# Two mixers' output projections in another order, with six of eight couples by seven products, in a float32 encoder trunk on one NeuronCore

## The chip, the cores and the metric

The program runs on one core of a Trainium2 chip. The metric is the device time of one execution in microseconds (us). The kernel before took 2365.94 us, the median of three runs (2365.79, 2365.94 and 2369.58). A further execution was recorded by the hardware profiler.

## What is computed

A two-layer encoder trunk over 256 tokens with model width 2048, in float32. Layer 0 mixes tokens with a bidirectional mLSTM (8 heads), layer 1 with a bidirectional HGRN2 (16 heads). Each mixer ends in an output projection, and a gated MLP of width 5504 follows:

```python
for layer in range(DEPTH):
    hn = rmsnorm(h, norm_mix_g[layer])
    mix = mlstm_mixer(hn, ...) if layer % 2 == 0 else hgrn_mixer(hn, ...)   # ends in y @ w_out
    h = h + mix
    h = h + conv_glu(rmsnorm(h, norm_ffn_g[layer]), ...)   # (gelu(conv(a)) * v) @ w_down, [a, v] = hn @ w_up
return rmsnorm(h, final_g)
```

The change concerns `y @ w_out` (a 256x2048 by 2048x2048 product, once in each layer), the residual add and the norm behind it, and the first product of the MLP.

## The kernel before

**Products.** Every large product is split into float32r parts: an operand `x` becomes `xh + xl`, a weight `wh + wl`, and three matmuls (h by h, h by l, l by h) stand for one float32 product. ScalarE (ACT) casts a raw weight piece to `wh` (L147), VectorE (DVE) subtracts to get `wl` (L148); a piece is 128x1024. TensorE (PE) runs a list of *chunks* one after another (`stream`, L324 on): "tm" chunks make 256 tokens by 512 columns (L373), "fm" chunks make 256 features by 256 tokens (L357 for h, L361 for l), and "st" chunks (*pairs*, L236) make 256 tokens by 1024 columns.

**Seven products.** A pair takes its k-tiles two at a time, as *couples* `u`: a 2x2 by 2x2 block product of 128x128 by 128x512 blocks. Directly that is eight block products, 24 matmuls of 128x512. For the couples listed in `seven`, it is done in seven block products, 21 matmuls, by a scheme of Strassen's kind. It needs four sums of blocks of `x` (`token_sums`, tiles `sx`, made on DVE and ACT) and four differences T1 to T4 of weight blocks. The eight accumulators hold four PSUM banks "mm" (P1, P6, P7, P5) and four "aux" (C11, C12, C21, C22). After the last couple by seven, `mid` (L581 on) adds P1, P6, P7, P5 to the residual `hm`; after the last couple, `done` adds C11 to C22 (L598).

**Weight differences.** They are made in one of two ways. `combine` (L202 on) makes them on DVE inside the pair (L207, four subtractions of 128x512). `prepare` (L613 on) makes them long before: it loads a couple of blocks into tiles `praw` (L621 or L395), subtracts four times (L633) and stores the result to DRAM `tscr` (L636); the pair then loads 768 KB into a tile `T` (L198), 768 KB of raw blocks (L135) and 256 KB from `tscr` (L199). `T` comes from `temporary`, with three buffers in the MLP's pool "ff" and two in the output projection's pool "op". A tile `T` is read by a cast and a subtraction of 1024 columns and by one of 512 columns, with one raw piece between.

**Who prepares what.** Each mixer stage prepares couples ahead (`prepare_early`): in layer 0 six, all for the MLP's first pair (`FIRST = 6`); in layer 1 nine, three for the mixer's own pair and six for the MLP. There the loads and stores go through the queue of SyncE (SP). The other couples of the MLP are prepared while its "up" chunks run; there loads and stores go through GpSimd (POOL). In all 63 couples are prepared; nine are combined inside a pair, three of them in layer 0's mixer, six in the MLPs (`FLY`).

**The output projection.** `mixed` (L656 on) makes four blocks of 512 columns of the residual: chunk `c0` (columns 0 to 511, tm), the pair `two` (columns 512 to 1535, couples 2, 4, 6 by seven, the other five by eight), then `c3` (columns 1536 to 2047, tm). The mixer's pool is closed and the pool "op" is opened when `c0` is done; "op" is closed before `c3`, and "ff" opens at the first up chunk.

**The norm behind it.** When a block of 512 columns of `hm` is complete, `Norm.add` (L420 on) squares it on ACT and queues `turn`: eight PE transposes in two groups (L434, tiles `pz`), then ACT and DVE split the four k-tiles `xt` (L379, L380). A `turn` that meets a running pair waits for it, or, where the pair has `ends`, for `mid`. After the fourth block the norm is finished (L417 to L460). The first up chunk needs `xt` 0 to 15 in order of k.

**Order.** The program text is turned into a queue of instructions for each engine by a list scheduler that simulates the engines at compile time; what is marked by `pin` or `late` keeps its program order on its engine. Side jobs (norms, preparations, heads of the mixers) are advanced by a clock `side.tick`, whose units are about 1 us in a tm chunk and about 0.54 us in an fm chunk. On the chip each engine runs its queue strictly in order.

Of the kernel before, what the change touches and what calls it, by code (L numbers as in the profile page):

```python
# [8 lines left out]
F32 = mybir.dt.float32  # L9
# [3 lines left out]
ALU = mybir.AluOpType  # L13
PSUM = bass.MemoryType.PSUM

P = 128
T = 256
D = 2048
KT = D // P
FT = 5504 // P  # L20
# [30 lines left out]
FLY = (2,), (5,), (2,), ()  # L51
FIRST = 6
SPLIT = (0, 2, 5), (0, 2, 5)
END = 3
SCRATCH = 4096
SEVEN_MIX = (2, 4, 6)

# [9 lines left out]
def trunk_kernel(ctx, tc, xT, x_d, fg_d, pp_d, cst_d, w_gate, w_first, w_aq, w_ak, w_av, w_ao, w_aout, w_ao2,  # L67
                 w_bq, w_bv, w_bg, w_bout, w_bo2, w_up, w_d0, w_d1, w_d3, out, mscr, tscr):
    nc = tc.nc
# [326 lines left out]


    class Norm:

        def __init__(self, gname, goff):  # L400
            self.g, self.o = gname, goff
            self.xs, self.rc_, self.R_ = [None] * KT, None, None

# [21 lines left out]
        def turn(self, c):  # L425
            yield 2.5
            while held and not held[-1].rest:
                yield 1.0
            for k0 in (4 * c, 4 * c + 2):
                pz = psm.tile([P, 512], F32, tag="mm", name="pz") if held else aux("pz")  # L430
                for k in (k0, k0 + 1):
                    for t in range(2):
                        o = (k - k0) * T + t * P
                        pe.transpose(pz[:, o:o + P], hm[:, t, k * P:(k + 1) * P], ident)  # L434
                for k in (k0, k0 + 1):
                    self.take(k, pz[:, (k - k0) * T:(k - k0 + 1) * T])
                yield 1.0
            if c == 3:
                self.total()
                self.finish()  # L440
                self.spread()
# [30 lines left out]
        def x(self, k):  # L472
            side.until(lambda: self.xs[k] is not None)
            return self.xs[k]

    class FinalNorm:
# [136 lines left out]
    def prepare(tiles, todo, first, period, finished, start, ahead):  # L613

        loaded = []

        def load(i):
            if i < len(todo):
                r = tiles(i)
                for j in range(2):  # L620
                    start(r[j], todo[i][0][:, j * 1024:(j + 1) * 1024])  # L621
                loaded.append(r)

        put = start if ahead else nc.sync.dma_start
        yield first
        load(0)
        if ahead:
            load(1)
        for i, (_, dst) in enumerate(todo):
            yield period / 2  # L630
            B11, B22, B21, B12 = (loaded[i][j // 2][:, j % 2 * 512:(j % 2 + 1) * 512] for j in range(4))
            for x, y, out in ((B12, B22, B22), (B12, B11, B12), (B11, B22, B11), (B21, B11, B21)):
                dve.tensor_tensor(out, x, y, ALU.subtract)  # L633
# [3 lines left out]
            if ahead:  # L637
                load(i + 2)
            yield period / 3
            if not ahead:  # L640
                load(i + 1)
        finished.append(True)
# [3 lines left out]
    def prepare_early(mp, layer, first, period):  # L646
        todo, finished = early[layer]
        side.push(prepare(lambda i: [mp.tile([P, 1024], F32, tag=f"p{j}", name="praw") for j in range(2)],
                          todo, first, period, finished, late, False))

# [4 lines left out]

    def mixed(w, w2, x, norm, close, layer=None):  # L656

        c0, _, _, c3 = project(lambda c: w[c // 3], KT, x, norm)
        op, SX, first = ExitStack(), {}, c0.done

        def sums(u):
            side.until(lambda: u in SX)
            return SX[u]

        two = pair(w2, KT, 1, x, sums, norm, SEVEN_MIX)
        if layer is not None:
            for u in SEVEN_MIX:
                store(two, w2, u, early[layer][0])
            two.waits = [early[layer][1]]

        def token():
            for i, u in enumerate(SEVEN_MIX):
                f = temporary(two.pool, "f")
                for j in range(2):
                    y = x(2 * u + j).bitcast(F32)
                    dve.tensor_tensor(f[:, j * T:(j + 1) * T], y[:, 0:T], y[:, T:2 * T], ALU.add)
                SX[u] = token_sums(two.pool, i, f[:, 0:T], f[:, T:2 * T], f[:, 2 * T:4 * T])
                yield 5.0

        def done(ps):  # L680
            side.drain()
            close()
            two.pool = op.enter_context(tc.tile_pool(name="op", bufs=1))
            two.pool.tile([P, LEAD], F32, name="lead")
            first(ps)
            side.push(token())

        c0.done, c3.before = done, op.close
        return [c0, two, c3]


    def mlstm(norm, nxt):
# [10 lines left out]
        box = {}  # L703
# [184 lines left out]
        for pr in range(AH // 2):  # L888
# [36 lines left out]
            def done_first(ps, done_v=done_v):  # L925
# [10 lines left out]
                side.push(start(gs))  # L936
                prepare_early(box["mp"], 0, 62.0, 25.0)

# [30 lines left out]

        return chunks + mixed(w_aout, w_ao2, yx, nxt, stack.close)  # L970


    def hgrn(norm, nxt):
# [4 lines left out]
        def begin():  # L978
            mp = box["mp"] = stack.enter_context(tc.tile_pool(name="hg", bufs=1))
            box["lv"] = mp.tile([P, 2 * P], F32, name="lv")  # L980
            late(box["lv"][:, 0:FINE * QUAD], cst_d[:, C_LV:])
            prepare_early(mp, 1, 30.0, 38.0)
            box["turn"] = 0
# [194 lines left out]
    def ffn(layer, norm, nxt):  # L1178
# [40 lines left out]
        for part, (f0, nf) in enumerate(((0, FA), (FA, FB))):  # L1219
# [96 lines left out]
def layout(x, norm_mix_g, norm_ffn_g, mlstm_w_in, mlstm_b_gate, mlstm_head_g, mlstm_w_out, hgrn_w_in, hgrn_lb,  # L1316
# [45 lines left out]
def build(nc, ins, out_shape=(2, P, D), **kw):  # L1362
# [3 lines left out]
    mscr = nc.dram_tensor("mscr", (64, T), F32, kind="Internal").ap()  # L1366
    tscr = nc.dram_tensor("tscr", (len(SEVEN_MIX) + 2 * sum(len(s) for layer in SEVEN for s in layer), P, 2048), F32, kind="Internal").ap()
    with tile.TileContext(nc, schedule_with_timeline_sim=True) as tc:
# [17 lines left out]
```

## Time and profile before

| | |
|---|---|
| median of three runs | 2365.94 us |
| the profiled execution | 2365.23 us |
| its span, first to last instruction | 2363.5 us |
| around the span | 1.7 us |
| mean granted TensorE clock | 0.999 |
| DMA traffic | 632.98 MB, mean 268 GB/s |

The span runs in stages: the first mixer to 299 us, its output projection to 388 us (`c0`, the pair from 322 to 364, `c3`), the MLP of layer 0 to 1081 us, the second mixer with its projection to 1664 us (the pair from 1597 to 1640), the MLP of layer 1 to the end. Times in the views are counted from the span's start. A PE row gives the duration of a single matmul from its start to its modelled end; matmuls overlap, so the pace of a series is read from starts, not from durations.

### The profile page before, as it was taken

The numbers are of one execution on the slowest core, as the hardware profiler recorded it, in microseconds if no ns is written. First come the engines' busy times: TensorE is split into PE (matmuls) and PEld (weight loads), VectorE is DVE, ScalarE is ACT, GpSimd is POOL, SyncE is SP. The second block draws the span as 40 slices with busy tenths as digits, with TensorE's granted clock in tenths as the row PEclk, the third lists the DMA queues.
The fourth block names the chain that finished last, engine by engine and source line by source line (L and its number), as shares of the span: only waits on it lengthen the run. The fifth ranks groups of instructions, "written<-read, shape, count | busy, mean of one in ns | idle before, by whom it ended". The sixth has DMA issues, their size and how long they took to land.

```text
span 2363.5 us, 38477 instructions
## 1 busy us (share of the span) xinstructions
PE 2353.8 (100%) x14545; PEld 2016.3 (85%) x14545; DVE 1992.4 (84%) x3087; ACT 1470.9 (62%) x2340; POOL 296.6 (13%) x436
## 2 busy tenths in 40 slices
PE   9999999999999999999999999999999999999998
PEld 8888888888888888888888888888888888888887
DVE  7777688997899998897888888778898789889787
ACT  7655455555665555676777777776555566455565
POOL 0100002110001110000232322221110000211000
PEclk9999999999999999999999999999999999999999
DMA  8776658985689996796656666557997588899695
GB/s 306 236 250 240 214 196 297 374 309 196 215 322 357 352 346 224 265 326 224 213 203 222 216 218 211 204 173 271 347 353 248 191 297 330 315 347 349 201 356 200
DMA packets 122267, 632.98 MB, mean 268 GB/s; under 512 B 13776, under 2 KB 14928, under 8 KB 77664
## 3 DMA queue, kind: packets, MB, share of 16 engines
q1 hardware_dynamic: 92736, 525.83, 62.7%
q0 software_dynamic: 28768, 103.89, 12.4%
q8 instruction: 114, 1.87, 0.3%
q10 hardware_dynamic: 576, 0.79, 0.1%
q14 instruction: 73, 0.60, 0.1%
HBM read 562.24 MB, written 68.22 MB: 267 GB/s over the span
## 4 chain that ended last, share of the span: by engine, by line
PE 98%; DVE 1%; issue 0%; DMA 0%; ACT 0%; POOL 0%; SPq 0%; POOLq 0%; DVEq 0%
PE mm L357 37%; PE mm L361 19%; PE mm L373 18%; PE pc L236 12%; PE mm L236 8%; PE pn L852 1%; PE py L1111 1%; PE pd L1061 0%; DVE wl L148 0%; PE pa L1061 0%; PE pz L434 0%; DMA raw<-in_w_first 0%; PE S L838 0%; ACT wh L147 0%; PE pz L1132 0%
## 5 line engine op out<-in xcount | busy, mean ns | idle before, releaser
L357 PE MATMUL mm<-xt,wh 128*128 128x512 f32 x3776 | 1312.4, 394 | 0.0
L148 DVE TENSOR_TENSOR wl<-raw,wh 128x1024 fp32r<-128x1024 f32 (+1 forms) x844 | 1037.1, 1234 | 231.0 <-ACT wh L147 224.0
L147 ACT CAST wh<-raw 128x1024 fp32r<-128x1024 f32 (+1 forms) x844 | 876.2, 1043 | 521.5 <-PE mm L357 307.1
L361 PE MATMUL mm<-xt,wl 128*128 128x256 f32 x3776 | 1043.4, 278 | 0.0
L357 PEld LDWEIGHTS mm<-xt,wh 128*128 128x128 f32 x3776 | 705.7, 188 | 161.1 <-issue 0.4
L361 PEld LDWEIGHTS mm<-xt,wl 128*128 128x128 f32 x3776 | 709.3, 188 | 4.5
L373 PE MATMUL mm<-wh,xt 128*128 128x512 f32 x1024 | 324.1, 392 | 0.2
L236 PE MATMUL pc<-wh,g 128*128 128x512 f32 (+1 forms) x716 | 243.1, 388 | 0.0
L373 PEld LDWEIGHTS mm<-wh,xt 128*128 128x128 f32 x1024 | 191.2, 188 | 39.4 <-ACT wh L147 0.5
L633 DVE TENSOR_TENSOR praw<-praw 128x512 f32<-128x512 f32 x252 | 173.4, 690 | 37.1 <-DMA praw<-in_w_d 28.0
L373 PE MATMUL mm<-wl,xt 128*128 128x512 f32 x512 | 199.9, 391 | 0.1
L236 PEld LDWEIGHTS pc<-wh,g 128*128 128x128 f32 x716 | 134.1, 188 | 27.9 <-ACT wh L147 0.4
L236 PE MATMUL mm<-wh,sx 128*128 128x512 f32 x432 | 153.6, 389 | 0.0
L148 DVE TENSOR_TENSOR wl<-T,wh 128x1024 fp32r<-128x1024 f32 (+1 forms) x144 | 136.3, 959 | 14.5 <-ACT wh L147 14.0
L147 ACT CAST wh<-T 128x1024 fp32r<-128x1024 f32 (+1 forms) x144 | 118.8, 835 | 45.7 <-DMA T<-tscr 11.8
L236 PE MATMUL pc<-wl,g 128*128 128x512 f32 (+1 forms) x358 | 138.8, 388 | 0.0
L373 PEld LDWEIGHTS mm<-wl,xt 128*128 128x128 f32 x512 | 96.2, 188 | 19.0 <-DVE wl L148 0.5
L621 POOL DMA_DIRECT2D praw<-in_w_d x96 | 51.6, 538 | 472.5 <-DMA tscr<-praw 269.6
L1074 DVE TENSOR_TENSOR QK<-QK,G 128x256 f32<-128x256 f32 x224 | 104.7, 515 | 6.2 <-ACT kq L1053 5.9
L1198 ACT COPY avc<-mm 128x256 f32<-128x256 f32 x172 | 64.0, 372 | 67.3 <-PE mm L361 67.3
L1053 ACT COPY kq<-QK 128x512 f32<-128x512 f32 x112 | 74.4, 669 | 36.2 <-DVE QK L1074 28.4
L236 PEld LDWEIGHTS mm<-wh,sx 128*128 128x128 f32 x432 | 81.1, 188 | 16.8
(248 smaller groups left out, 2326.0 us busy)
## 6 DMA issues: line engine op xcount, KB each, us to landing
raw<-in_w_up SPq DMA_DIRECT2D x172, 1024.0 KB, 7.2
praw<-in_w_d POOLq DMA_DIRECT2D x96, 512.0 KB, 7.8
tscr<-praw POOLq DMA_DIRECT2D x96, 512.0 KB, 7.9
raw<-in_w_bq SPq DMA_DIRECT2D x48, 1024.0 KB, 5.0
T<-tscr SPq DMA_DIRECT2D x63, 768.0 KB, 7.5
raw<-in_w_d SPq DMA_DIRECT2D x60, 768.0 KB, 5.9
raw<-in_w_ao SPq DMA_DIRECT2D x24, 1024.0 KB, 4.8
raw<-in_w_d SPq DMA_DIRECT2D x24, 1024.0 KB, 6.8
```

What stands on the lines that cost most here:

```text
L147: pin(act.copy(wh[:, :m], r))
L148: pin(dve.tensor_tensor(wl[:, :m], r, wh[:, :m].bitcast(F32), ALU.subtract))
L236: pin(pe.matmul(ps, a, b, start=bank not in begun, stop=stop and i == 2))
L357: hold(pe.matmul(ps[f], wh[:, c:c + P], x, start=k + kk == 0, stop=False))
L361: hold(pe.matmul(ps[f][:, 0:T], wl[:, c:c + P], x[:, 0:T], start=False, stop=k + kk == ch.nk - 1))
L373: pe.matmul(ps[t], x[:, a + t * P:a + (t + 1) * P], w[:, c], start=st and i == 0, stop=sp and i == 2)
L621: start(r[j], todo[i][0][:, j * 1024:(j + 1) * 1024])
L633: dve.tensor_tensor(out, x, y, ALU.subtract)
L852: pe.matmul(pn[:, 0:258], w, v, start=(i == 0), stop=(i == len(parts) - 1))
L1053: act.copy(m, blocks(QK, h))
L1074: dve.tensor_tensor(two[:, j], two[:, j], by[:, j], ALU.mult)
L1198: act.copy(z, p[:, T:2 * T])
```

## The change

- In `mixed`, the list becomes `[c0, c3, two]`: the pair is last. Couples 1 to 6 go by seven products (before 2, 4, 6), in both layers, and all their differences come from `tscr`. The pool "op" closes when the pair is done, and the pair has `ends`.
- The pair's columns are now last in the norm, so the first k-tiles that the MLP can have are 0 to 3 and 12 to 15. The up chunks walk the k-tiles in that `ORDER`, and the weights `w_up` are laid out to match.
- The first mixer's preparation makes ten couples (six for its own pair, four for the MLP), sends loads and stores through POOL in pinned order, and starts and paces earlier. The second mixer's makes twelve, by SP as before.
- The MLP of layer 0 prepares two couples more in its first part (14 instead of 12). All preparations during up chunks pin their subtractions and POOL transfers, and have a shorter period.

```diff
-FIRST = 6
+FIRST = 4, 6
-SEVEN_MIX = (2, 4, 6)
+SEVEN_MIX = (1, 2, 3, 4, 5, 6)
+ORDER = (0, 1, 2, 3, 12, 13, 14, 15, 4, 5, 6, 7, 8, 9, 10, 11)
...
+    def aside(dst, src):
+        tc.keep_in_program_order(pool.dma_start(dst, src))
...
-            if c == 3:
+            self.left -= 1
+            if not self.left:
                 self.total()
...
+        def ordered(self, k):
+            return self.x(ORDER[k])
...
-        put = start if ahead else nc.sync.dma_start
+        own = start is aside
+        put = start if own else nc.sync.dma_start
+        hold = pin if own else lambda ins: ins
         yield first
-        load(0)
-        if ahead:
-            load(1)
+        for i in range(ahead):
+            load(i)
...
-                dve.tensor_tensor(out, x, y, ALU.subtract)
+                hold(dve.tensor_tensor(out, x, y, ALU.subtract))
...
-                          todo, first, period, finished, late, False))
+                          todo, first, period, finished, late if layer else aside, 1))
...
-        if layer is not None:
-            for u in SEVEN_MIX:
-                store(two, w2, u, early[layer][0])
-            two.waits = [early[layer][1]]
+        for u in SEVEN_MIX:
+            store(two, w2, u, early[layer][0])
+        two.waits, two.ends, last = [early[layer][1]], True, two.done
...
-                yield 5.0
+                yield 3.4
...
-        c0.done, c3.before = done, op.close
-        return [c0, two, c3]
+        def end(ps):
+            last(ps)
+            op.close()
+
+        c0.done, two.done = done, end
+        return [c0, c3, two]
...
-                prepare_early(box["mp"], 0, 62.0, 25.0)
+                prepare_early(box["mp"], 0, 52.0, 15.0)
...
-            prepare_early(mp, 1, 30.0, 38.0)
+            prepare_early(mp, 1, 24.0, 34.0)
...
-                                  todo, 18.0, (nf * 10.4 - 26.0) / len(todo), finished, pool.dma_start, True))
+                                  todo, 18.0, (nf * 10.4 - 26.0) / len(todo) - 2.5, finished, aside, 2))
...
-                chunks.append(Chunk("fm", w_up[layer, f0 + i], KT, norm.x, done_up(f0 + i, i, GT, SX, SEVEN[layer][part]),
+                chunks.append(Chunk("fm", w_up[layer, f0 + i], KT, norm.ordered, done_up(f0 + i, i, GT, SX, SEVEN[layer][part]),
...
-            chunks.append(two(w0, 0, nxt if part else None, seven, fly, (0, 0, n) if part else (FIRST, n - FIRST)))
+            chunks.append(two(w0, 0, nxt if part else None, seven, fly, (0, 0, n) if part else (FIRST[layer], n - FIRST[layer])))
...
-    up = A(ffn_w_up).reshape(2, KT, P, 2, FT, P).transpose(0, 4, 2, 1, 3, 5)
+    up = A(ffn_w_up).reshape(2, KT, P, 2, FT, P)[:, list(ORDER)].transpose(0, 4, 2, 1, 3, 5)
```

More of the change, by code (lines that the diff above doesn't have):

```diff
@@ L401, in __init__ @@
             self.g, self.o = gname, goff
-            self.xs, self.rc_, self.R_ = [None] * KT, None, None
+            self.xs, self.rc_, self.R_, self.left = [None] * KT, None, None, 4
         def take(self, k, src, g=None, *pin):
@@ L636, in prepare @@
                 put(dst[:, j * 1024:(j + 1) * 1024], loaded[i][j])
-            if ahead:
-                load(i + 2)
+            if own:
+                load(i + ahead)
             yield period / 3
-            if not ahead:
-                load(i + 1)
+            if not own:
+                load(i + ahead)
         finished.append(True)
@@ L654, in store, with mixed @@
         todo.append((src[:, 2048 * u:2048 * (u + 1)], ch.stored[u]))
-    def mixed(w, w2, x, norm, close, layer=None):
+    def mixed(w, w2, x, norm, close, layer):
         c0, _, _, c3 = project(lambda c: w[c // 3], KT, x, norm)
@@ L968, in yx @@
             return YT[k]
-        return chunks + mixed(w_aout, w_ao2, yx, nxt, stack.close)
+        return chunks + mixed(w_aout, w_ao2, yx, nxt, stack.close, 0)
     def hgrn(norm, nxt):
@@ L1366, in build @@
     mscr = nc.dram_tensor("mscr", (64, T), F32, kind="Internal").ap()
-    tscr = nc.dram_tensor("tscr", (len(SEVEN_MIX) + 2 * sum(len(s) for layer in SEVEN for s in layer), P, 2048), F32, kind="Internal").ap()
+    tscr = nc.dram_tensor("tscr", (2 * len(SEVEN_MIX) + 2 * sum(len(s) for layer in SEVEN for s in layer), P, 2048), F32, kind="Internal").ap()
     with tile.TileContext(nc, schedule_with_timeline_sim=True) as tc:
```

## The prediction

> **What bounds the kernel now.** First the page, then PE's own waits, then the chain of waits.
>
> ```profile
> span 2363.5 us, 38477 instructions
> PE 2353.8 (100%) x14545; PEld 2016.3 (85%) x14545; DVE 1992.4 (84%) x3087; ACT 1470.9 (62%) x2340; POOL 296.6 (13%) x436
> PE 98%; DVE 1%; issue 0%; DMA 0%; ACT 0%; POOL 0%; SPq 0%; POOLq 0%; DVEq 0%
> ```
> ```profile
> PE idle L1269 <- POOL ones L1262: 1.1, 1, 1.1
> PE mm L236 <- DVE wl L148: 0.3, 1, 0.3
> ```
>
> The second fence is the whole list of PE's waits: 1.4 us in 2363.5, of which 0.3 us behind the start. PE runs from end to end, and 98% of the chain lies on it. So an edit counts here only if it changes PE's list of instructions or makes PE wait. The engines next in load (DVE 84%) matter only where they make a tile late.
>
> What does one matmul cost? The page gives some 390 ns, but this is a duration from start to end, and matmuls overlap. The chain of waits through the first mixer's pair gives the pace:
>
> ```profile
> 322.40 10.88 PE pc L236 x48
> ```
>
> 48 matmuls of 128x512 advance the chain by 10.88 us: **0.2267 us each**. The whole pair (five couples of 24 and three of 21, 183 matmuls) would be 41.5 us by this, and the windows show that it is:
>
> ```profile
> 322.40:363.90 41.50, 41.50 (x185) 34.37 (x184) 36.23 (x44) 23.84 (x29) 0.00 (x0) 1.00 0.57 196
> 634.00:742.00 108.00, 107.69 (x474) 88.48 (x473) 99.07 (x110) 72.83 (x86) 4.81 (x5) 1.00 0.85 322
> 1596.70:1639.90 43.20, 43.20 (x193) 35.71 (x192) 36.07 (x53) 24.28 (x31) 0.00 (x0) 1.00 0.70 246
> ```
>
> (Columns: stretch, length, then busy time and count of PE, weight loads, DVE, ACT, POOL, then clock, DMA share and GB/s.) The mixers' pairs hold no slack to recover. The only hole in the rows above is 0.31 us in the MLP's pairs of layer 0.
>
> **The change, part by part.**
>
> *Seven products.* Three couples more in each of two layers, three matmuls less for each: 18 x 0.2267 = **-4.08 us**. All other chunks keep their matmuls, and the norms their transposes. No reordering can bring much beside it: the holes behind the start are 0.3 us, and I bound what smoother joints between chunks could add by 1 us in all.
>
> *The differences arrive in T.* This is the part that can give the gain back. In the new pair six couples in a row take a tile T, which has two buffers in this pool. The nearest rows are the same six steps in the MLP's last pair of layer 0, which has three buffers:
>
> ```profile
> 1062.10 1.05 ACT L147 CAST wh<-T 128x1024 fp32r<-128x1024 f32 x1 [0.40 <-DMA T<-tscr]
> 1062.94 0.39 PE L236 MATMUL mm<-wh,sx 128*128 128x512 f32 x1
> 1065.46 0.68 DVE L148 TENSOR_TENSOR wl<-T,wh 128x512 fp32r<-128x512 f32 x1
> 1067.70 0.39 PE L236 MATMUL mm<-wh,sx 128*128 128x512 f32 x1
> ```
>
> From T's first cast to the end of its last reader are 1062.10 to 1066.14, 4.04 us: so long a buffer is held. PE's first matmul with T2 stands at 1067.70 (the one before, at 1062.94, belongs to the couple before: 4.76 us = 21 x 0.2267). So the cast was 5.6 us early. It needs to be 2.3 us early (cast 1.05, subtraction 1.2), so 3.3 us are slack. Then the load:
>
> ```profile
> DMA to landing us min/median/max: 4.0/7.5/10.1
> DMA to landing us min/median/max: 4.0/8.0/9.2
> DMA to landing us min/median/max: 4.5/5.6/6.9
> ```
>
> These are T's loads in the whole run, in that pair (975 to 1080 us), and in the second mixer's pair (1590 to 1640 us, three loads, every second couple). With two buffers, a buffer comes round every 2 x 4.76 = 9.52 us, and needs 4.04 + 7.5 = 11.54 at the median: 2.02 us late per round. T1 and T2 are loaded ahead, beside `c3`; T3 and T4 are 2.0 late, T5 and T6 are 4.0 late, against 3.3 of slack: PE waits 0.7 us once, about couple 5. With 8.0 us it would be 1.7, with 5.6 none, with the longest, 10.1, 5.9. I take the median, since these couples load as densely as the MLP's: 768 + 768 + 256 KB, 1.835 MB in 4.76 us, are 385 GB/s, where the best-loaded window below reached 354 at a share of 0.94. Cost: 2 x 0.7 = **+1.4 us**, bounds 0 and 11.8.
>
> The Trainium skill, page "DMA: Bandwidth & Descriptors", section "Anatomy of one DMA — SWDGE (gpsimd) path", fits a transfer by 2.0 us plus bytes over 436 GB/s; that gives an estimate of 3.8 us for T alone and 6.2 us with its couple's other loads in front of it. The least landing above, 4.0, agrees with the first, the median of 7.5 lies over both. By this page T would never be late enough, and the sum would be the clean rival's below.
>
> *The pair last, the norm behind it.* Formerly four k-tiles were missing when the up chunk began, needed after twelve others; now eight are missing, needed after eight. At the old joint:
>
> ```profile
> 388.27 0.39 PE L357 MATMUL mm<-xt,wh 128*128 128x512 f32 x1
> 391.08 0.40 PE L357 MATMUL mm<-xt,wh 128*128 128x512 f32 x1
> ```
> ```profile
> 390.14 0.68 DVE L550 TENSOR_TENSOR hm<-hm,mm 128x512 f32<-128x512 f32 x1
> 394.96 0.47 DVE L380 SCALAR_TENSOR_TENSOR xt<-pz,pp,xt 128x256 fp32r<-128x256 f32 x1
> ```
>
> Two starts four k-tiles apart give 0.70 us per k-tile. The first late tile was ready at 395.43, 7.2 us after the joint; it was due after 12 x 0.70 = 8.4 plus eight transposes. Now it is due after 5.6 us plus transposes (about 0.11 us each, up to eight ahead of it): some 6.5. If the same delay held, PE would wait 0.7 us; with none of the transposes ahead of it, 1.6. But of the pair's four sums the first tiles need only C11 and C21, whose last matmuls stand 18 and 6 before the end: 4.1 and 1.4 us earlier than the last. I take **0**, bounds 0 and 1.6 for each joint. If its cover (the eight tiles of `ORDER` 0 to 3 and 12 to 15) is missing, because `turn` of `c3` waits for `mid` and that is late, the whole chain of 7 us is bare.
>
> *DVE and ACT.* Nine couples more are prepared, four subtractions of 684 ns each; three `combine`s go, four of the same kind:
>
> ```profile
> L633 DVE TENSOR_TENSOR praw<-praw x252: 672/684/1311, 96.6 to 2173.8; 128x512 f32<-128x512 f32 x126
> 53.00:322.00 269.00, 269.00 (x1381) 228.94 (x1380) 201.92 (x382) 154.26 (x252) 15.76 (x25) 1.00 0.69 228
> 388.30:470.00 81.70, 81.70 (x476) 71.48 (x475) 71.78 (x120) 47.07 (x75) 14.15 (x26) 1.00 0.94 354
> 363.90:388.30 24.40, 24.40 (x121) 20.23 (x121) 22.60 (x34) 15.61 (x28) 7.96 (x12) 1.00 0.94 337
> ```
>
> Four couples more in the first mixer are 11 us on a DVE that was free for 67 of 269 us; two more in layer 0's MLP 5.5 us, beside up chunks where PE never waited; three more in the second mixer 8 us. `c3` carried 22.6 us of DVE work in 24.4; four of those were preparation for the MLP that had moved forward and now stays behind. The sums `sx` take that place. Cost 0 while DVE stays a few pieces ahead; bound: the cover is three pieces, 8 us of PE.
>
> *Queues.* SP loses 24 issues in the first mixer. In the second it gets three couples more, 12 issues. POOL gets 40 in the first mixer, each load behind the landing of the store before it; who stands behind them are `Mb` and the powers `rs` (L541). I cost this at 0, and its failure is the last rival. In the MLPs the shorter period asks for more than POOL's loop of load, subtract, store gives, so the transfers keep their own pace:
>
> ```profile
> POOL praw L621 <- DMA tscr<-praw: 269.6, 73, 10.8
> tscr<-praw POOLq DMA_DIRECT2D x96, 512.0 KB, 7.9
> ```
>
> **Sum.** -4.08 + 1.4 + 0 = -2.7 us. The profiled execution took 2365.23 us (span 2363.5 and 1.7 around it), so 2362.5; it lies 0.7 below the median of the runs shown, 2365.94, on which I set the forecast: **2363.2 us**.
>
> **The rivals.**
>
> 1. *Clean.* T lands in the 5.6 us of the second mixer's pair, nothing waits: 2365.94 - 4.08 = 2361.9, down to 2360.9 with 1 us from the joints. For it: those rows are of the same place and buffers. Against it: there every second couple had a T.
> 2. *Given back.* T takes 8.0 us (1.7 a layer, 3.4), both joints wait 1.6 (3.2): -4.08 + 6.6 = +2.5, 2368.5. For it: the MLP's pair above had that median of 8.0, with loads as dense.
> 3. *Slower: POOL's order in the first mixer.* Ten couples make POOL wait for stores, 7.9 us at a time, and a power `rs` behind one is late by up to that; DVE, in order, stops at L875 and makes no `wl`.
>
> ```profile
> 92.58 0.72 POOL L541 TENSOR_TENSOR rs<-rs,mhalf 128x2 f32<-128x2 f32 x1 [8.76 <-DVE rs L540]
> 162.79 2.00 POOL L541 TENSOR_TENSOR rs<-rs,mhalf 128x2 f32<-128x2 f32 x2 [15.65 <-DVE rs L540]
> ```
>
> Three or four powers fall into the stretch of the preparation. PE's cover is 8 us when full; if half of it is there, each costs 4 us, and above one hit the gain is lost; three give -4.08 + 1.4 + 12 = +9.3, 2375.2. Against it: the scheduler puts instructions where its simulation sees no wait, and POOL idles most of this stage.
> 4. *Not what it says*: without the 18 matmuls nothing is left to gain, 2365.9.
>
> **How the numbers follow.** Forecast, 0.42 (own range 2361.5 to 2366); clean 0.27; given back 0.16; slower 0.13; nothing removed 0.02. Runs of this kernel can tell apart about 0.2%, 4.7 us; -4.08 alone stays inside that. Faster by more needs the clean case with at least 0.6 us from the joints: 0.17, and 0.05 for a lucky order elsewhere: 0.22. Slower by more is rival 3 and a bad tail of rival 2: 0.14. The rest, 0.64, is within. The range leaves some 0.06 below 2360.6 and 0.13 above 2369.5.
>
> **What would show it.** The pairs' windows: 174 matmuls, 39.4 us if clean; a wait of PE on `wl` or of ACT on `T<-tscr` about couples 3 to 6 shows the buffers. At the joint: PE waiting on `xt` eight k-tiles into the first up chunk. In the first mixer: DVE waiting on POOL `rs`. The prediction is wrong if PE's list of waits grows by more than 5 us, or if the time falls by more than the 18 matmuls and 1 us.

## The result, and the profile after

The changed kernel takes **2391.8 us** (median of four runs, 2389.46 to 2394.87), the kernel before 2367.07 (four runs, 2365.79 to 2369.58). The ratio is 1.0105, with a 95% interval from 1.0093 to 1.0117: slower by 1%, and outside the range that was forecast. The profiled execution took 2392.63 us.

From the page of the changed kernel, the span, the busy times and the shares of the chain by engine:

```profile
span 2390.5 us, 38653 instructions
PE 2364.9 (99%) x14527; PEld 2019.2 (84%) x14527; DVE 2026.6 (85%) x3165; ACT 1480.1 (62%) x2358; POOL 317.6 (13%) x484
PE 88%; DMA 5%; DVE 4%; issue 2%; ACT 1%; POOL 0%; SPq 0%; POOLq 0%; DVEq 0%; ACTq 0%
```

PE has 14527 matmuls, 18 fewer than before, and yet the span grew by 27.0 us. The chain, which lay on PE for 98%, now leaves it for DMA and DVE. PE's waits, which were two rows, begin like this:

```profile
PE mm L358 <- DVE xt L381: 6.1, 6, 1.8
PE mm L362 <- DVE wl L149: 3.2, 2, 1.9
PE pn L865 <- ACT Wh L856: 1.7, 2, 1.4
PE mm L374 <- DVE wl L149: 1.4, 2, 0.8
```

(Columns: total us, times, longest. In this kernel the casts stand at L148, `wl` at L149, the fm matmuls at L358 and L362, tm at L374, the split of `xt` at L381, the preparation's subtractions at L643 and its POOL transfers at L400.)

To see where the 27.0 us arise, I cut both spans at the same places of the program: first mixer (up to its last chunk, a tm chunk of 28 us), that chunk and the projection together, up stage of layer 0, rest of that MLP, second mixer with its projection, up stage of layer 1, rest. First the windows of the kernel before, of which four are needed:

```profile
29.70:271.80 242.10, 242.10 (x1270) 206.89 (x1267) 181.72 (x331) 143.87 (x237) 16.84 (x29) 1.00 0.73 246
271.80:388.30 116.50, 116.50 (x554) 97.35 (x553) 97.24 (x158) 67.29 (x106) 9.35 (x14) 1.00 0.61 213
388.30:633.90 245.60, 245.60 (x1422) 214.76 (x1421) 209.94 (x342) 140.15 (x223) 21.11 (x39) 1.00 0.79 281
1664.40:1910.00 245.60, 245.60 (x1421) 214.73 (x1420) 210.14 (x343) 139.92 (x223) 21.06 (x39) 1.00 0.79 279
```

Then those of the changed kernel:

```profile
30.60:283.20 252.60, 246.78 (x1271) 209.66 (x1268) 181.50 (x337) 143.86 (x236) 35.00 (x63) 0.99 0.73 252
283.20:399.10 115.90, 114.44 (x536) 94.65 (x535) 96.85 (x163) 69.52 (x106) 4.95 (x8) 1.00 0.72 255
399.10:651.40 252.30, 249.11 (x1430) 217.09 (x1429) 224.92 (x370) 143.81 (x233) 34.19 (x59) 0.99 0.87 306
651.40:1098.50 447.10, 446.71 (x2294) 379.72 (x2292) 402.33 (x545) 276.42 (x382) 39.74 (x56) 1.00 0.85 303
1098.50:1680.40 581.90, 581.44 (x4978) 497.40 (x4979) 482.21 (x810) 409.24 (x759) 131.96 (x177) 1.00 0.65 227
1680.40:1936.20 255.80, 251.90 (x1428) 217.63 (x1427) 221.12 (x363) 143.33 (x233) 29.96 (x51) 1.00 0.83 287
```

Three places carry the loss: the **first mixer +10.5**, the **up stage of layer 0 +6.7**, the **up stage of layer 1 +10.2**. The rest of the first MLP takes 447.1 us in both. The second mixer with its projection went from 583.4 to 581.9 (-1.5). The second row of each fence went from 116.5 to 115.9 (-0.6), and two changes hide in it. The mixer's last chunk went from 27.7 to 30.2 us (+2.5), with 1.46 us without a matmul; that belongs to the first mixer's loss. The projection itself went from 88.8 to 85.7 (-3.1), as it lost nine matmuls worth 2.04 us and eight transposes, which the up stage has now (1430 instead of 1422).

**First mixer.** Here DVE is in trouble, not PE. DVE's waits for data of the preparation, in the kernel before (90 to 290 us) and in the changed one (90 to 300 us):

```profile
DVE praw L633 <- issue: 2.1, 1, 2.1
DVE praw L633 <- DMA praw<-in_w_d: 1.2, 1, 1.2
```
```profile
DVE praw L643 <- DMA praw<-in_w_ao: 21.2, 4, 7.9
DVE praw L643 <- issue: 10.4, 2, 6.9
DVE praw L643 <- DMA praw<-in_w_d: 6.4, 1, 6.4
```

3.3 us have become 38 us, in seven stops: four of 6.4 to 7.9 us and three of 2.5 to 3.5, all in front of the preparation's first subtraction of a couple. (For two of them, the row "issue", the profile names nothing that was waited for; they end 7.6 and 4.8 us after the couple's last load was issued.) One of the seven in DVE's timeline, and in POOL's (a row is start, duration, engine, line, operation, and in brackets what the engine waited for):

```profile
187.41 1.23 DVE L149 TENSOR_TENSOR wl<-raw,wh 128x1024 fp32r<-128x1024 f32 x1 [1.55 <-ACT wh L148]
196.51 0.69 DVE L643 TENSOR_TENSOR praw<-praw 128x512 f32<-128x512 f32 x1 [7.87 <-DMA praw<-in_w_ao]
198.39 1.22 DVE L149 TENSOR_TENSOR wl<-raw,wh 128x1024 fp32r<-128x1024 f32 x1
```
```profile
179.24 0.54 POOL L400 DMA_DIRECT2D tscr<-praw  x1 [10.56 <-DVE praw L643]
187.15 0.53 POOL L400 DMA_DIRECT2D praw<-in_w_ao  x1 [6.65 <-DMA tscr<-praw]
190.22 0.53 POOL L400 DMA_DIRECT2D praw<-in_w_ao  x1 [2.54 <-DMA tscr<-praw]
```

There is one set of `praw` tiles. A couple's store is issued at 179.2; the load of the next couple has to wait for that store (to 187.15), and DVE gets the data at 196.5, some 17 us after the store was issued. The subtraction is pinned in DVE's queue for an earlier time, so DVE stands still for 7.9 us, and the next `wl` is made 11.0 us after the last. PE's cover is a little shorter:

```profile
197.34 0.39 PE L358 MATMUL mm<-xt,wh 128*128 128x512 f32 x1
199.66 0.39 PE L362 MATMUL mm<-xt,wl 128*128 128x256 f32 x1 [1.93 <-DVE wl L149]
200.23 0.63 PE L358 MATMUL mm<-xt,wh 128*128 128x512 f32 x1
```

The last row shows a second price. After this stop of 1.9 us a matmul takes 0.63 instead of 0.39 us, for 3.4 us. The windows of that stretch, and of a like one behind the first joint, have a granted clock of 0.50 (third number from the end):

```profile
200.20:203.60 3.40, 3.40 (x13) 2.92 (x12) 3.40 (x7) 2.30 (x3) 0.89 (x2) 0.50 0.90 282
411.90:415.20 3.30, 3.30 (x12) 2.82 (x12) 1.12 (x4) 0.16 (x2) 2.49 (x5) 0.50 0.87 299
```

A pair of matmuls (h and l) takes 0.64 us there instead of 0.35, so such a stretch costs some 1.6 us. There are two of them in the first mixer. So of its 10.5 us, 5.8 are holes, that is time without a matmul (252.60 - 246.78), some 3 are half clock, and the remaining 1.5 are not traced.

**The joints.** Where the pair ends and the up stage begins, POOL and DVE of the changed kernel show:

```profile
401.59 1.29 POOL L600 TENSOR_TENSOR hm<-hm,u 128x512 f32<-128x512 f32 x1 [82.75 <-DVE u L599]
402.85 2.26 POOL L601 TENSOR_TENSOR hm<-hm,u 128x512 f32<-128x512 f32 x1
```
```profile
396.56 2.35 DVE L149 TENSOR_TENSOR wl<-raw,wh 128x1024 fp32r<-128x1024 f32 x2
400.82 0.68 DVE L599 TENSOR_TENSOR u<-u,mm 128x512 f32<-128x512 f32 x1
402.01 1.94 DVE L149 TENSOR_TENSOR wl<-raw,wh 128x1024 fp32r<-128x1024 f32 x1
404.67 1.27 DVE L607 TENSOR_TENSOR hm<-hm,pc 128x512 f32<-128x512 f32 x2
408.94 1.65 DVE L381 SCALAR_TENSOR_TENSOR xt<-pz,pp,xt 128x256 fp32r<-128x256 f32 x4
```

The end of `mid` (L599) stands in DVE's queue behind `wl` pieces and is done at 401.5, when the up stage has already run for 2 us. Then come POOL's two sums (3.5 us). The `wl` that begins while the first sum runs takes 1.94 instead of 1.22, and the second sum, which begins while that `wl` runs, takes 2.26 instead of 1.29. Behind them stand C21 and C22 on DVE, the transposes, and from 408.94 on the splits of the last `xt`, for which PE waits at 409.47 and 411.39. In the kernel before, the chunk `c3` lay over all this. The Trainium skill, page "SBUF — State Buffer", section "Who interferes with whom", says that a DVE instruction with two SBUF inputs contends with a GpSimd one that reads SBUF; the rows at 402.01 and 402.85 agree.

PE's waits at each joint make some 3.2 us (399.1 to 651.4) and 3.9 us (1680.4 to 1936.2), by the holes in the windows above. With 8 and 7 more transposes (0.11 us each) and one half-clock stretch, 5.7 of the 6.7 us of layer 0 are accounted for. In layer 1 there is no half-clock stretch, so waits and transposes give only 4.7 of 10.2. The rest is something that no wait shows:

```profile
1700.00:1900.00 200.00, 200.00 (x1156) 174.83 (x1156) 172.55 (x284) 113.69 (x185) 13.95 (x27) 1.00 0.76 266
```
```profile
1700.00:1900.00 200.00, 200.00 (x1134) 173.35 (x1133) 174.88 (x283) 109.81 (x174) 22.49 (x42) 1.00 0.85 297
```

The first window is of the kernel before, the second of the changed one. Both are without a hole and at clock 1.00, inside the same stage, and one has 1156 matmuls, the other 1134. In PE's timeline a pair takes **346.7 ns** in the one and **353.3 ns** in the other, evenly through the stage. The slow pace does not begin at a stop: after the last wait (1693.4 us) the pairs still take 347 ns, and they turn slow at 1698 us, behind four small products of the norm, which the kernel before has in this stage too, at 1675.9 us, without turning slow. From there to the end are 238 us, 674 pairs; 6.7 ns each make **4.5 us**, and with them 9.2 of the 10.2 are accounted for.

### The profile page after: what moved, and what is told of

It reads as the page before. It is cut to its first block, busy times and chain, and to the rows that moved or that the text cites. A ratio compares the mean times of both kernels' runs of the same rounds, so it can differ in the third digit from the quotient of the medians.

```text
span 2390.5 us, 38653 instructions
## 1 busy us (share of the span) xinstructions
PE 2364.9 (99%) x14527; PEld 2019.2 (84%) x14527; DVE 2026.6 (85%) x3165; ACT 1480.1 (62%) x2358; POOL 317.6 (13%) x484
## 4 chain that ended last, share of the span: by engine, by line
PE 88%; DMA 5%; DVE 4%; issue 2%; ACT 1%; POOL 0%; SPq 0%; POOLq 0%; DVEq 0%; ACTq 0%
PE mm L358 35%; PE mm L362 18%; PE mm L374 15%; PE pc L237 9%; PE mm L237 7%; DVE wl L149 2%; DMA T<-tscr 2%; DMA tscr<-praw 2%; DMA praw<-in_w_d 1%; DMA praw<-in_w_ao 1%; PE py L1124 1%; PE pn L865 1%; ACT wh L148 1%; PE pd L1074 0%; PE pa L1074 0%
## 5 line engine op out<-in xcount | busy, mean ns | idle before, releaser
L358 PE MATMUL mm<-xt,wh 128*128 128x512 f32 x3776 | 1321.3, 396 | 7.0 <-DVE xt L381 6.1
L149 DVE TENSOR_TENSOR wl<-raw,wh 128x1024 fp32r<-128x1024 f32 (+1 forms) x844 | 1034.3, 1231 | 209.8 <-ACT wh L148 203.1
L148 ACT CAST wh<-raw 128x1024 fp32r<-128x1024 f32 (+1 forms) x844 | 875.2, 1043 | 516.3 <-PE mm L358 340.5
L362 PE MATMUL mm<-xt,wl 128*128 128x256 f32 x3776 | 1048.0, 279 | 3.2 <-DVE wl L149 3.2
L358 PEld LDWEIGHTS mm<-xt,wh 128*128 128x128 f32 x3776 | 707.4, 188 | 172.1 <-DVE xt L381 7.7
L362 PEld LDWEIGHTS mm<-xt,wl 128*128 128x128 f32 x3776 | 711.7, 189 | 9.3 <-DVE wl L149 3.8
L374 PE MATMUL mm<-wh,xt 128*128 128x512 f32 x1024 | 323.7, 392 | 1.0 <-ACT wh L148 0.9
L643 DVE TENSOR_TENSOR praw<-praw 128x512 f32<-128x512 f32 x288 | 200.0, 694 | 47.4 <-DMA praw<-in_w_ao 21.2
L374 PEld LDWEIGHTS mm<-wh,xt 128*128 128x128 f32 x1024 | 191.5, 188 | 40.5 <-ACT wh L148 1.4
L374 PE MATMUL mm<-wl,xt 128*128 128x512 f32 x512 | 200.3, 392 | 1.4 <-DVE wl L149 1.4
L149 DVE TENSOR_TENSOR wl<-T,wh 128x512 fp32r<-128x512 f32 (+1 forms) x156 | 147.8, 958 | 25.4 <-ACT wh L148 25.0
L237 PE MATMUL mm<-wh,sx 128*128 128x512 f32 x468 | 166.9, 390 | 0.0
L148 ACT CAST wh<-T 128x512 fp32r<-128x512 f32 (+1 forms) x156 | 128.8, 835 | 59.1 <-DMA T<-tscr 29.6
L400 POOL DMA_DIRECT2D tscr<-praw x120 | 64.5, 538 | 525.0 <-DVE praw L643 493.3
L374 PEld LDWEIGHTS mm<-wl,xt 128*128 128x128 f32 x512 | 96.3, 188 | 21.1 <-DVE wl L149 2.3
L237 PEld LDWEIGHTS mm<-wh,sx 128*128 128x128 f32 x468 | 87.7, 188 | 18.4 <-ACT wh L148 0.5
```

The lines of the kernel that those rows point to most:

```text
L148: pin(act.copy(wh[:, :m], r))
L149: pin(dve.tensor_tensor(wl[:, :m], r, wh[:, :m].bitcast(F32), ALU.subtract))
L237: pin(pe.matmul(ps, a, b, start=bank not in begun, stop=stop and i == 2))
L358: hold(pe.matmul(ps[f], wh[:, c:c + P], x, start=k + kk == 0, stop=False))
L362: hold(pe.matmul(ps[f][:, 0:T], wl[:, c:c + P], x[:, 0:T], start=False, stop=k + kk == ch.nk - 1))
L374: pe.matmul(ps[t], x[:, a + t * P:a + (t + 1) * P], w[:, c], start=st and i == 0, stop=sp and i == 2)
```

## The experiments

My theory after the first reading: two independent losses, (1) the preparation's single set of tiles, which stops DVE in the first mixer, and (2) the bare joint behind the pair. Rivals: (3) the pairs themselves suffer (T too late), (4) one cause for all, the denser traffic of ten couples. T can be set aside from the trace. PE has no wait at all in the first pair (340 to 399 us) and one of 0.2 us, for a `wl`, in the second, and T's loads land in these times there (four loads) and in the second pair (1610 to 1680, six):

```profile
DMA to landing us min/median/max: 4.5/6.9/7.6
DMA to landing us min/median/max: 4.4/6.5/8.6
```

**The old order with the new preparation (a3)**, and **the new order alone (a4).**

```diff
-SEVEN_MIX = (1, 2, 3, 4, 5, 6)      # a3
+SEVEN_MIX = (2, 3, 4, 5, 6)
-        return [c0, c3, two]
+        return [c0, two, c3]
```
```diff
-        return [c0, two, c3]           # a4, on the kernel before
+        return [c0, c3, two]
```

Both with the `ORDER`, `ends` and closing of the pool that belong to the order.

> The changed kernel with the old order (c0, pair, c3), k-tiles in their natural order, and couples 2 to 6 by seven (couple 1 cannot be, its T would be wanted before the pool opens). Theory 2 (the pair in last place lays bare a chain of sums on DVE and POOL, transposes and splits, 8 us at the first joint and 10.7 at the second): both joints go, 2391.8 - 18.7 + 1.4 for two couples by eight = about 2374. Rival (it is the six couples with two buffers T that cost it): stays within 3 us of 2391.8 or falls by less than 6.

> The kernel before with the order alone changed: c0, c3, pair, k-tiles 0 to 3 and 12 to 15 first; couples 2, 4, 6 by seven and all preparation as before. Theory 2: both joints cost what they cost in the changed kernel, about +18, 2385. Rival (the joints cost only where DVE is behind because of six couples by seven): within 4 us of 2367.

a3: 2386.46 us, ratio 1.0081 [1.0064, 1.0098]. That is 5.3 us less than the changed kernel, not the 18 expected; by its time alone it is what the rival said ("falls by less than 6"), and only the windows decide. Both up stages were back at 245.5 us, so the joint is what they paid; the first mixer kept its stops. But the second pair took 49.4 us, where as many products would take some 41.7 at the pace of the kernel before: 3.6 us are waits for `wl`, `wh` and once (1.0 us) for `sx`, and one half-clock stretch is among the rest. T was not late there (ACT waited 0.3 us for its loads). a4: 2382.02 us, 1.0057 [1.0041, 1.0074], near the 2385 expected: the order alone, without any further couple, costs 15 us. Its up stages are 4.2 and 10.8 us longer, about 1 us of each by the transposes that moved there, and another 5.6 lie in the second part of layer 1's MLP, where PE stops twice for a `wl` (1.9 us) and runs at the slower pace after it. So (1) and (2) are separate, and (4) does not explain the joints.

**The preparation at another pace (a1), with the old order (a5), and with other shares (b2, b6, c1).** A longer period should let the subtractions meet data that has landed; fewer couples for the MLP should make room.

```diff
-                prepare_early(box["mp"], 0, 52.0, 15.0)
+                prepare_early(box["mp"], 0, 52.0, 25.0)    # a1, a5, b2, b6, c1
-FIRST = 4, 6
+FIRST = 0, 6      # b2, b6: six couples in the first mixer; c1: 2, 6
```

b6 and c1 take couples 0 to 5 by seven as well (b5, below); b2 and b6 hold the MLP's period at 11.9 or more.

> The changed kernel with one number of the first mixer's preparation: a period of 25 side units instead of 15. Theory 1 (DVE, in order, stops at pinned subtractions whose load on POOL's queue has not landed, because store and load take some 14 us and the text leaves about 7 us of an up-like chunk): with 25 units the stops go, the stage from 178 to 283 us gets its 10 us back, 2391.8 becomes about 2381. Rival (POOL's queue itself, powers and Mb behind the stores, whatever the pace): under 2 us gained, about 2390.

> Old order, couples 2 to 6 by seven, and period 25 in the first mixer. Theories 1 and 2 together: 10 matmuls... twelve matmuls less than before (2.7 us) and no stall, about 2364. If something else of the change costs time (POOL pinned, the MLP's shorter period, the longer lists), it stays above 2368.

> The changed kernel with only its own six couples prepared in the first mixer, period 25; the four of the MLP are made in the MLP (18 there, period not below 11.9 side units as in the changed kernel). Theory 1 as the runs left it (one set of tiles praw gives a couple about every 20 us: a shorter period stops DVE, ten couples at a longer one end after the stage does): six fit at 25, neither stop, 2391.8 - 10.6 = about 2381. If 18 couples are too many for the MLP, its pair waits for the last of them and the time stays above 2386.

> Couples 0 to 5 by seven and the preparation of the run with six couples in the first mixer. If the two costs are separate, their gains add: about 2391.8 - 10.6 - 8 = 2373, still above the kernel before's 2367 by what is left of the joints.

> Couples 0 to 5 by seven, one set of tiles praw, eight couples in the first mixer at period 25, 16 in the MLP. By the pace seen (about 25 us a couple from 97 us on) the eighth ends at about 340 us, where the pair's pool can open in time; 16 at 13.8 us end at about 632, just before the MLP's pair. If both hold: 2370. Rival: one of the two ends late, 2378 or more.

Results: a1 2405.47 us (1.0162 [1.0147, 1.0178]), a5 2397.47 (1.0125 [1.011, 1.014]), b2 2400.26 (1.0136 [1.0121, 1.0151]), b6 2392.91 (1.0099 [1.0084, 1.0114]), c1 2379.51 (1.0046 [1.0029, 1.0063]). In all of them DVE's stops in the first mixer go, as expected, or nearly (0.9 us is left in c1), and the wait comes back elsewhere. PE's waits of a1 (300 to 420 us) and of b2 (600 to 760 us) each have one row that carries it:

```profile
PE mm L237 <- ACT wh L148: 18.6, 3, 17.2
```
```profile
PE pc L237 <- ACT wh L148: 10.6, 1, 10.6
```

In a1 the store of the tenth couple, issued at 364 us, has landed at 368, and only then may the pair's pool open and T be loaded; the pair began at 346. In a5 the pair waits 12.8 us for `sx`. In b2 and b6 the mixer and its pair are clean, and the MLP's pair, whose 18 couples come one every 14 us, waits instead (16.9 us without a matmul in b2; from that pair to the second projection both kernels are 23 us longer than the changed kernel). With one set of tiles a couple takes some 20 us in the first mixer, so ten of them don't fit without stops: what is not paid on DVE is paid at the pair. In c1 the first projection takes 97.2 us, 11.4 more than in c3 below, as its rival said (one of the two ends late, 2378 or more). My expectations for a1, a5, b2 and b6 were wrong by 19 to 34 us, as they counted only the stops that go.

**A second set of tiles (c2).** If the round trip is the cause, a couple loaded one step ahead into other tiles must take the stops away at the same pace. Four tiles of 512 columns that are free in this stage (`yt12` to `yt15`) serve every second couple.

```diff
+        def tiles(i):
+            if layer or i % 2 == 0:
+                return [mp.tile([P, 1024], F32, tag=f"p{j}", name="praw") for j in range(2)]
+            return [keep.tile([P, 512], F32, tag=f"yt{KT - 4 + j}", name="praw") for j in range(4)]
+        side.push(prepare(tiles, todo, first, period, finished, late if layer else aside, 1 if layer else 2))
```

> The changed kernel with a second set of tiles praw in the first mixer (four tiles of 512 columns in slots that are free until the last heads), so that the load of a couple is issued while the couple before is worked on; ten couples, period 15. Theory 1 (DVE stops because one set of tiles gives a store and a load, some 14 us, between two couples): the stops go without the lateness of longer periods, the first mixer gets 8 to 11 us back, 2391.8 becomes 2381 to 2384. Rival (any preparation by POOL in pinned order at this pace stops DVE): within 3 us of 2391.8.

2376.48 us, 1.0027 [1.0015, 1.0038]: 15.3 us less than the changed kernel, where 8 to 11 were expected. DVE's waits for `praw` are gone, and the first mixer's window is:

```profile
29.90:272.10 242.20, 242.20 (x1271) 206.84 (x1268) 189.43 (x343) 143.88 (x237) 46.09 (x85) 1.00 0.79 272
```

That is the 242.1 us of the kernel before, with nine of the ten couples made there instead of six (DVE 7.7 us busier). The extra gain lies in the mixer's last chunk, 27.7 instead of 30.2 us, since the stops behind 283 us were of the same kind, and in the half-clock stretch of layer 0's joint, which did not occur, though PE had the same four stops there. Loss (1) is shown, with its size: 10.4 us in the mixer and 2.5 in its last chunk. The DMA traffic of this window is denser than in the changed kernel (272 instead of 252 GB/s), so (4) falls here too. What the pin costs by itself was not tried.

**The joint: POOL's sums on DVE (b1), and an earlier last couple by seven (b5).**

```diff
-            pool.tensor_tensor(part(1, 0), part(1, 0), u, ALU.add)    # b1
-            pool.tensor_tensor(part(1, 1), part(1, 1), u, ALU.add)
+            dve.tensor_tensor(part(1, 0), part(1, 0), u, ALU.add)
+            dve.tensor_tensor(part(1, 1), part(1, 1), u, ALU.add)
```
```diff
-SEVEN_MIX = (1, 2, 3, 4, 5, 6)
+SEVEN_MIX = (0, 1, 2, 3, 4, 5)    # b5
```

In b5 two couples by eight stand behind `mid` instead of one, 5.4 us more for its sums.

> The changed kernel with the two sums that mid puts on POOL (1.3 and 2.3 us, one after the other) made on DVE instead (0.7 us each). Theory 2a (at the joint the last two sums of the residual, C21 and C22, and the squares stand behind these POOL sums): each joint gets some 2 to 4 us back, 2391.8 becomes 2384 to 2388. Rival 2b (DVE itself is the queue, three subtractions wl in a row stand before the sum with P7): DVE gets 1.2 us more per joint, 2391 to 2394.

> The changed kernel with couples 0 to 5 by seven instead of 1 to 6: same number of matmuls, but mid comes one couple (5.4 us) earlier, so P1 to P7, the POOL sums and the four k-tiles of c3 are off the joint. Theory 2 (the joint is a chain that starts at mid): 3 to 5 us back at each joint, 2382 to 2386. Rival (it starts at the last matmul, with C21 and C22): within 2 us of 2391.8.

b1: 2388.53 us, 1.0082 [1.0067, 1.0097], 3.3 less than the changed kernel, between theory 2a and rival 2b. Its holes at the two joints are 6.0 us instead of 7.1, and its up stages take 250.1 and 255.6 us; a repeat of the unaltered changed kernel (d1, below) took 250.0 and 257.1. So moving POOL's sums changes the waits at the joints by 1 us at most (in d1 the holes are 6.7 us without it), and the rest of the 3.3 is not shown to be the joints'. b5: 2381.98 us, 1.0055 [1.0034, 1.0077], 9.8 less, at the lower end of what was expected. Its two up stages take 247.4 and 250.2 us, instead of 252.3 and 255.8.

**Both mended (c3), and b1's edit on top (c5).**

> The second set of tiles and couples 0 to 5 by seven. The two gains (about 10 and 9.8 us, the second as measured) add if the costs are separate: 2370 to 2374.

> The same, with the two POOL sums of mid on DVE as well. With mid a couple earlier, POOL's sums should be off the joint, so this is worth nothing more or 1 us less: 2370 to 2375. If it gains 3 us again, POOL's sums still stand in the joint.

c3 (c2 with couples 0 to 5): 2366.83 us (ten runs, 2366.14 to 2367.97), the kernel before beside it 2369.86 (25 runs, 2364.66 to 2373.72), ratio 0.9991 [0.9982, 1.0001]: no difference that can be told. It is 3 to 7 us below what was expected; the gains as measured one by one, 15.3 (c2) and 9.8 (b5), add up to it. c5: 2369.62, 0.9999 [0.999, 1.0009], 2.8 above c3: once `mid` is earlier, POOL's sums on DVE gain nothing. The windows of c3 for the mixer's last chunk with the first projection, and for the two up stages:

```profile
272.40:385.90 113.50, 113.50 (x537) 94.89 (x536) 95.24 (x163) 69.18 (x107) 8.11 (x8) 1.00 0.70 243
385.90:633.20 247.30, 246.69 (x1429) 215.59 (x1428) 220.36 (x364) 143.19 (x230) 30.91 (x58) 1.00 0.87 308
1661.60:1911.80 250.20, 248.19 (x1429) 216.72 (x1427) 217.26 (x357) 142.71 (x231) 28.01 (x51) 0.99 0.83 287
```

So with both causes mended 24.8 of the 27.0 us of span are gone (2390.5 to 2365.7). What the 18 matmuls save is given back at the up stages, which are still 1.7 and 4.6 us longer than before. In the second, 2.0 are waits on `xt`, 0.8 transposes, and some 1.5 a half-clock stretch at 1672 us.

**Is the slower pace a property of the program (d1 to d4)?** The 4.5 us of layer 1 are in the first profile of the changed kernel, and the fast pace is in b5's and c3's. Before crediting the couples with it I profiled three of the kernels again, unaltered: d1 and d2 are the changed kernel, d3 is a4, d4 is b5.

> The changed kernel, a second profiled execution of the same program. In the first one the whole up stage of layer 1 ran at 353.3 ns per h and l pair of matmuls, where the kernel before, and the changed kernel's other up stages, show 346.7 ns at the same granted clock of 1.00. Theory A (the pace belongs to the program, set by how PE stops at that joint): 353.3 ns again, the stage 255 to 256 us, span within 1.5 us of 2390.5. Theory B (the pace is drawn anew at each restart of PE, in each execution): in some executions 346.7 ns, then the stage takes some 251 us and the span some 2386; another stage may be slow instead.

> The changed kernel, a third profiled execution. As for the run before: A expects the stage of layer 1 at 353.3 ns a pair in this one too; B expects that among these repeats at least one stage shows another pace than in the first execution.

> The kernel before with the order alone, run again. In its first profile both up parts of layer 1 ran at 353.4 ns a pair (from 1660 us, and again from 2140 us). A: both again, span within 1.5 us of 2382.1. B: at least one of the two at 346.7 ns, which takes 4.6 us off for the first and 3.9 us for the second; its four executions so far were 2375.7, 2380.9, 2383.1 and 2383.9 us, which B reads as different numbers of slow parts.

> Couples 0 to 5, run again. In its first profile all up parts ran at 346.7 ns a pair, the up stage of layer 1 took 250.2 us. A: the same, 250 us, so that the earlier last couple by seven is what brings the fast pace. B: the pace is not tied to the couples, and this stage can show 353.3 ns and some 255 us; then of the 9.8 us that this edit took off in the median about half was the pace, and the rest the joint.

Times: 2390.35, 2393.03, 2383.96 and 2384.41 us. In layer 1, the slow pace came again in d1, d2 and d3, and the fast one in d4. Here are the windows of d1, and of d4 in layer 0 and layer 1:

```profile
1700.00:1900.00 200.00, 200.00 (x1134) 173.53 (x1133) 174.87 (x284) 111.07 (x176) 22.55 (x42) 1.00 0.85 297
```
```profile
420.00:620.00 200.00, 200.00 (x1134) 173.45 (x1133) 178.38 (x292) 110.33 (x177) 26.73 (x50) 1.00 0.89 312
1700.00:1900.00 200.00, 200.00 (x1157) 174.90 (x1156) 178.57 (x293) 112.67 (x179) 22.47 (x42) 1.00 0.85 300
```

But d4 has the slow pace in layer 0, where the same program ran fast in b5 (1155 matmuls in these 200 us). So neither theory holds alone. In layer 1 the pace went with the joint: slow in all profiles of the changed kernel, a4, b1, b2 and c2, whose last couple by seven is 6, and fast in all five kernels with couples 0 to 5, and in the kernel before, a1, a3 and a5 (of these a1 has couple 6 last too, and the same five stops of 0.3 to 1.8 us at the joint as the changed kernel, so neither the couple nor the stops decide). In layer 0 it can differ from one execution to the next; there b6 was slow too. In a4 it also switched inside a stage: fast until PE's stop of 1.48 us for a `wl` at 2096.8 us, slow after it. So the pace is settled where the alternation has been broken, by a stop or by other products, and stays until the next break. Of the 9.8 us that b5 gained, up to 4.5 are pace, and that part is not safe, as d4 shows. What decides between the two paces stays open; it was not tried by itself. The half-clock stretch, too, differs between executions of one program: the changed kernel has it at layer 0's joint in its first profile and in d2, and at layer 1's (clock 0.61 from 1690.5 to 1693.9 us) in d1.

## Why the prediction was wrong

- **The matmuls, -4.08.** Right in mechanism: 18 fewer, and the pairs ran at their pace, with one wait of 0.2 us. c3's first projection is 3.0 us shorter (85.8 instead of 88.8), 2.04 by matmuls and 0.9 by the transposes that moved out of it.
- **T, +1.4 (0 to 11.8).** Mis-sized; it measured 0. The loads landed in 6.9 and 6.5 us at the median, not in 7.5, and no wait of PE is put down to them. By the prediction's own sum 6.9 us makes T5 and T6 2.8 us late, inside the slack of 3.3. The term, and rival 2's first half, fall. "Clean" had it right that nothing waits, though not by the landing of 5.6 that it gave. The fit that the prediction takes from the Trainium skill is, by the section that it names, for transfers issued from GpSimd; T is loaded through SP's queue.
- **"Cost 0 while DVE stays a few pieces ahead".** This step failed first. It counted DVE's busy time (11 us more, against 67 free) and not its order. The cover was named rightly ("three pieces, 8 us of PE"), but the wait that uses it up was not: a subtraction pinned in DVE's queue in front of a load that has not landed. Seven stops of 2.5 to 7.9 us cost 10.4 us of span in the mixer and 2.5 in its last chunk, and c2 takes them away.
- **"Queues ... I cost this at 0, and its failure is the last rival".** Rival 3 was the right stage and the right chain (store, load on POOL, DVE in order, no `wl`), at the wrong instruction. It put the stop at the powers `rs` and L875, and DVE waited for a power 1.6 us in all. The quoted row "POOL praw L621 <- DMA tscr<-praw: 269.6, 73, 10.8" already told that a load waits for the store, 3.7 us on average and up to 10.8; I read it as POOL's idleness, and did not ask for whom DVE would wait once the subtraction is pinned. Its "against", that the scheduler puts instructions where it sees no wait, failed: in the order it made, the subtraction stands ahead of its load's landing on the chip, time after time.
- **The joints, 0 (0 to 1.6 each).** The cover was said to be the eight tiles, "if ... that is late, the whole chain of 7 us is bare"; that happened. I took the delay after the last sum from the old joint, where the pair's `mid` and POOL's sums had ended long before under `c3`. In the new joint they stand on the path: `mid` behind several `wl`, then 3.5 us of POOL. Of these two, b5 and c3 show that an earlier `mid` helps (+1.7 and +4.6 are left), and b1 that POOL's part is small. Measured +6.7 and +10.2, of which 3.2 and 3.9 are waits; the rest are transposes, half clock, and the slower pace. The last two are prices that the prediction did not know, and what brings them on is not settled.
- **The range.** Its upper end let one loss happen. Two independent ones happened, and the half clock and the slower pace came on top of the stops.

## What to carry to other kernels

An instruction that is pinned in the queue of an engine that feeds the bottleneck needs its data there early: count the round trip of the tile it uses (here store, then load, some 17 us with one set) against its period, and give it a second set before giving it a denser schedule. When a chunk is moved to the end of a stage, list all that used to run under the chunk that followed it, through every engine's queue, since that work is on the path from then on. Where PE runs without a break, allow for a stop that costs more than its length, and profile a kernel more than once before crediting an edit with a few us.

## What the runs showed of the hardware

- A stop of PE of 1.9 us (and four of 0.4 to 1.1 us in a row, at 401 to 411 us) was followed by a stretch of 3.4 us at a granted clock of 0.50, worth some 1.6 us. Not every such stop is: c2 has the same four stops and stays at 1.00, and the five of 0.3 to 1.8 us at layer 1's joint (1682 to 1694 us) bring no stretch in the first profile and one in d1. The Trainium skill, page "TensorE: Matmul & The Clock Gate", section "Part 1: The HAM clock gate (the "warmup" mystery)", gives a window of 3413 ns, which the length agrees with, and idleness of a whole window as the condition; here stops shorter than that sufficed.
- At clock 1.00 the same alternation of 512- and 256-column matmuls has two steady paces, 346.7 and 353.3 ns a pair, settled at a break and kept for up to 240 us.
- A sum of 128x512 on POOL took 1.29 us where it began before a `wl` subtraction on DVE, and that `wl` 1.94 instead of 1.22; a sum that began while the `wl` ran took 2.26.
